# Quarter sums of a fast up-projection: formed in DRAM ahead of time, or by accumulating loads onto the raw weight buffers

## The chip, the cores and the metric

The kernel runs on one core of a Trainium2 chip. The metric is the device time of one execution in microseconds (us). Engines are named as in the profile: PE (TensorE), DVE (VectorE), ACT (ScalarE), POOL (GpSimd) and SP (SyncE). DMAs are issued from SP (plain loads and stores) and from POOL (transfers that add to what lies at the destination, and the copies that go with them).

## The reference, cut to what matters

The program is an encoder of two layers over 512 tokens with 1024 channels. Each layer has a mixing half (one input projection, a convolution, three kinds of attention, gates, an output projection) and a feed-forward half. The change is in the feed-forward half:

```python
def _conv_ffn(h, w_up, conv_w, conv_b, w_down):
    u = _depthwise_conv(h @ w_up, conv_w, conv_b)      # w_up: 1024 x 5632
    gate, up = jnp.split(u, 2, axis=-1)                # 2 x 2816 columns
    return (jax.nn.silu(gate) * up) @ w_down
...
x = x + _conv_ffn(_rmsnorm(x, g_ffn[l]), w_up[l], ffn_conv_w[l], ffn_conv_b[l], w_down[l])
```

## The kernel before, in words

**Units.** All weights come in units of 128 x 1024 float32 (512 KB). `weights` (lines 225 to 254) loads a unit into a raw buffer by a DMA on SP (line 246), ACT writes its rounded high part `w_hi` (line 250), and DVE writes the remainder `w_lo = w_raw - w_hi` (line 252). A product is three matmuls (high by high, high by low, low by high). `unit` keeps two units ahead of the one in use (`LOOK = 2`), and `w_hi` and `w_lo` have three buffers each. So the split of a unit can begin when PE is done with the unit three places earlier. There are two raw buffers `w_raw`; the feed-forward half has two more under the tag `w_more`.

**The up-projection.** Its 5632 output columns are worked in 11 groups g of 512 (two blocks of 128 gate columns and the two blocks of up columns that go with them). Groups 0, 1 and 7 to 10 are computed plainly: four units each, called whole units (`block`, lines 289 to 296), of 24 matmuls with 512 columns. Groups 2 to 6 (`SEVEN`) use a fast scheme with seven products instead of eight: the weights of a group are cut into four quarters A11, A12, A21, A22 (rows and columns of a 2 x 2 split), and the seven products use the three quarters A11, A12, A22 and four sums S1 to S4 of quarters. `seven` (lines 972 to 1020) does one of them: 24 matmuls with 256 columns (line 989), then what ACT and DVE have to do with the result. In sums, with the signs already in the packed weights:

- S3 = A11 + A21, S2 = S3 + A22, S4 = S2 + A12
- S1 = A22 + A21

**Where the sums come from.** `quarter_sums` (lines 1111 to 1132) makes them in DRAM. For each of the five groups and each of the four sums POOL issues one DMA that copies 512 KB and one that adds another 512 KB: 40 DMAs for a layer. `weights` then loads a sum like any other unit (`w_raw<-qS`).

**Work in the background.** The down-projection uses a scheme of the same kind, and its sums are also made in DRAM: `weight_sums` (lines 1134 to 1161), 24 POOL DMAs for a layer of up to 1 MB each, into the tiles `sums`. Both generators stand in one chain in the list `slow`, the quarter sums first (line 1432). `tick` (lines 877 to 895) is called several times in each piece of PE work. It adds `pace` to an account, and while the account is positive it takes the next DMA from the list, which costs 4 for a quarter sum and 11 for a weight sum. Each such DMA waits for the last matmul issued so far (`paced`), so that it starts at its place in PE's work. `pace` is 4.0 and then 2.7 in the mixing half, 0.8 in the seven-product groups, and 2.7 in the whole groups that follow (lines 1062 and 1065).

**The order of the up-projection** is the list `UP_STEPS` (lines 39 to 53): one group after the other, in a seven-product group S3, A11, A22, S2, A12, S1, S4; the last product of a group stands behind the first of the next.

**Behind the up-projection.** The result of a step goes from PSUM through `U` (line 1069 for whole units) and `conv_part` (lines 1022 to 1047) to the gated products `f`, and `split_pair` (lines 1180 to 1217) prepares those for the down-projection. `down` (line 1219) starts with units that hold a quarter of `w_down` and one of the sums (`w_raw<-sums`), and its first products need four PSUM banks of the kind `mm`, the ones that the last up units used.

Of the kernel before, what the change touches and what calls it, by code (L numbers as in the profile page):

```python
# [14 lines left out]
F32 = mybir.dt.float32  # L15
F32R = mybir.dt.float32r
# [6 lines left out]
P = 128  # L23
# [15 lines left out]
def up_steps():  # L39

    steps, held = [], []
    for g in range(NP2):
        if g in SEVEN:
            own = [('seven', g, n) for n in ('S3', 'A11', 'A22', 'S2', 'A12', 'S1', 'S4')]
        else:
            own = [('whole', 2 * g + i, s) for i in range(2) for s in range(2)]
        steps += own[:1] + held
        held = own[-1:] if g in SEVEN else []
        steps += own[1:len(own) - len(held)]
    return steps  # L50
# [166 lines left out]
class Trunk:  # L217
# [7 lines left out]
    def weights(self, upto, ahead=3000, parts=1, queue=None):  # L225

        nc = self.nc
        while self.w_emitted < min(upto, len(self.w_list)):
            n, pieces = self.w_list[self.w_emitted]
            with self.tc.high_priority(offset=ahead):  # L230

                self.w_fast = (self.w_fast + 1) % 4 if n < 2 else 0
                if n == 0 and self.w_fast in (3, 0) or n == 1 and self.w_fast % 2 == 1:
                    raw = self.fp.tile([P, 1024], F32, name="w_raw", tag="w_more", bufs=2)
                else:
                    raw = self.wpool.tile([P, 1024], F32, name="w_raw", tag="w_raw", bufs=2)
# [812 lines left out]
    def ffn(self, l, last):  # L1049
# [9 lines left out]
        self.seven_forms()  # L1059
        for kind, a, b in UP_STEPS:  # L1060
            if kind == 'seven':
                self.pace = 0.8
                self.seven(a, b)
            else:
                self.pace = 2.7 if a > 2 * SEVEN[-1] else 0.0
                ps = self.mm()
                self.block(ps)
                self.tick()
                v.tensor_tensor(self.U[b][:, a % 2, 1:513], ps, self.RB, ALU.mult)  # L1069
# [41 lines left out]
    def quarter_sums(self, l):  # L1111

        dma = lambda *a, **k: self.paced(self.nc.gpsimd.dma_start(*a, **k))  # L1113
        q, t = self.quarters[l], self.qsums[l]
        for g in SEVEN:
            for n in ('S1', 'S2', 'S3', 'S4'):
                t[g, n] = self.dram.tile([P, 1040], F32, name=f"q{n}{g}", tag=f"q{n}{g}", bufs=2)[:, :1024]
        for n, a in (('S3', (1, 0)), ('S1', (1, 1))):
            for g in SEVEN:
                dma(t[g, n], q[(g,) + a])  # L1120
                yield 4
        for n, a in (('S3', (0, 0)), ('S1', (1, 0))):
            for g in SEVEN:
                dma(t[g, n], q[(g,) + a], accum_op=ALU.add)
                yield 4
        for n, m, a in (('S2', 'S3', (1, 1)), ('S4', 'S2', (0, 1))):
            for g in SEVEN:
                dma(t[g, n], t[g, m])
                yield 4
            for g in SEVEN:  # L1130
                dma(t[g, n], q[(g,) + a], accum_op=ALU.add)
                yield 4
# [193 lines left out]
    def run(self):  # L1326
        nc, tc = self.nc, self.tc
        with ExitStack() as st:
# [8 lines left out]
            self.quads, self.sums, self.all_quads, self.quarters, self.qsums = [], [], [], [], []  # L1337
            self.halves = {}
            for l in range(L):
                off, quads, quarters, ups, sums = 0, [], {}, {}, {}  # L1340
# [11 lines left out]
                for kind, a, b in UP_STEPS:  # L1352
                    if kind == 'whole':
                        self.w_list.append((1024, lambda src=ups[b * DFF + a * P]: [src]))
                    elif b[0] == 'A':
                        self.w_list.append((1, lambda src=quarters[a, int(b[1]) - 1, int(b[2]) - 1]: [src]))
                    else:
                        self.w_list.append((1, lambda s=sums, at=(a, b): [s[at]]))
                self.quarters.append(quarters)
                self.qsums.append(sums)  # L1360
# [52 lines left out]
    def layer(self, l):  # L1413
# [3 lines left out]
        with tc.tile_pool(name="gate", bufs=1, reuse_waits="tile") as self.gp:  # L1417
            with tc.tile_pool(name="attn", bufs=1, reuse_waits="tile") as self.ap:
# [13 lines left out]
                self.slow.append(chain(self.quarter_sums(l), self.weight_sums(l)))  # L1432
# [102 lines left out]
```

## Time and profile before

| | before |
|---|---|
| runs, us | 1571.79, 1564.55, 1564.35 |
| median, us | 1564.55 |
| the profiled execution's own time, us | 1565.39 |
| its span in the profile, us | 1563.6 |
| PE busy in the span, us | 1542.8 |
| DVE busy, us | 1250.6 |
| ACT busy, us | 894.0 |
| moved by DMA, MB | 306.84 |

The span runs from the first to the last instruction, and the execution's own time is 1.8 us longer. PE counts as busy while a matmul is under way, and its matmuls overlap: one with 256 columns shows 283 ns and starts about 120 ns after the one before. The granted clock of PE stands in the windows view; 1.00 is full speed. The time of a DMA "to landing" runs from its issue on SP or POOL to the event that tells that it is complete.

### The profile page before, as it was taken

To read this page: it belongs to the slowest core of one execution; us is meant where nothing else is said; L and a number is where in the kernel's file an instruction comes from. 1 tells how busy PE (TensorE), PEld (TensorE's weight loads), DVE (VectorE), ACT (ScalarE), POOL (GpSimd) and SP (SyncE) were. 2 spreads that over 40 slices of the span, in tenths; PEclk is the share of its full clock that TensorE was granted. 3 is DMA by queue.
4 is the path that set the end of the run, shared out by engine and by line. 5 is a ranking of instruction groups with operands and counts; after the bars stand their busy time and mean duration, and the time that the engine had idled before them with its cause. 6 is when DMAs were issued, how large, how long until landed. Compare 5 with 4: busy or idle time off the path is not lost.

```text
span 1563.6 us, 21943 instructions
## 1 busy us (share of the span) xinstructions
PE 1542.8 (99%) x7842; PEld 1310.0 (84%) x7842; DVE 1250.6 (80%) x2114; ACT 894.0 (57%) x1504; POOL 203.4 (13%) x308
## 2 busy tenths in 40 slices
PE   9999999999999999989999999999999999999998
PEld 8888888888789998868888878888888899988787
DVE  6689988764789997986576889887646899999764
ACT  6678767333456664554457677673334566645543
POOL 0133002222100000000002231032221000000000
PEclk9999999999999999999999999999999999999999
DMA  7787765557845868696558977655578469886874
GB/s 239 250 238 211 160 167 156 161 145 164 239 164 145 254 217 162 182 259 203 183 179 272 233 197 158 171 148 169 145 166 249 166 168 276 247 193 181 234 238 160
DMA packets 124797, 306.84 MB, mean 196 GB/s; under 512 B 28176, under 2 KB 30096, under 8 KB 124688
## 3 DMA queue, kind: packets, MB, share of 16 engines
q1 hardware_dynamic: 93712, 212.10, 41.7%
q0 software_dynamic: 30688, 92.81, 28.1%
q8 instruction: 62, 1.02, 0.3%
q10 hardware_dynamic: 288, 0.52, 0.1%
q14 instruction: 47, 0.39, 0.1%
HBM read 287.56 MB, written 100.67 MB: 248 GB/s over the span
## 4 chain that ended last, share of the span: by engine, by line
PE 79%; DVE 9%; DMA 7%; ACT 4%; issue 1%; POOL 0%; ACTq 0%; DVEq 0%; POOLq 0%; SPq 0%
PE mm L272 14%; PE mm L271 14%; PE mm L273 14%; PE aux L989 10%; DMA w_raw<-W 4%; DVE w_lo L252 3%; PE aux L1226 2%; PE aux L1227 2%; PE aux L1228 2%; PE mm L500 2%; PE mm L502 2%; PE mm L501 2%; PE mm L1227 2%; PE mm L1226 2%; PE mm L989 2%; PE mm L1228 2%
## 5 line engine op out<-in xcount | busy, mean ns | idle before, releaser
L250 ACT ACTIVATE w_hi<-w_raw 128x1024 fp32r<-128x1024 f32 (+1 forms) x335 | 350.5, 1047 | 391.0 <-PE mm L272 137.4
L252 DVE TENSOR_TENSOR w_lo<-w_raw,w_hi 128x1024 fp32r<-128x1024 f32 (+1 forms) x335 | 405.9, 1212 | 124.3 <-ACT w_hi L250 122.2
L271 PE MATMUL mm<-xh,w_hi 128*128 128x512 f32 x960 | 375.3, 391 | 1.2 <-DVE V L628 1.2
L273 PE MATMUL mm<-xh,w_lo 128*128 128x512 f32 x960 | 374.4, 390 | 0.3 <-DVE w_lo L252 0.3
L272 PE MATMUL mm<-xl,w_hi 128*128 128x512 f32 x960 | 374.2, 390 | 0.0
L273 PEld LDWEIGHTS mm<-xh,w_lo 128*128 128x128 f32 x960 | 180.2, 188 | 39.6 <-DVE w_lo L252 1.5
L271 PEld LDWEIGHTS mm<-xh,w_hi 128*128 128x128 f32 x960 | 180.3, 188 | 38.0 <-DVE V L628 1.6
L272 PEld LDWEIGHTS mm<-xl,w_hi 128*128 128x128 f32 x960 | 180.3, 188 | 36.0
L989 PE MATMUL aux<-form,w_hi 128*128 128x256 f32 x640 | 116.3, 283 | 0.1
L989 PEld LDWEIGHTS aux<-form,w_hi 128*128 128x128 f32 x640 | 99.9, 192 | 0.5 <-ACT sv L1001 0.3
L438 DVE SCALAR_TENSOR_TENSOR cv<-cv,prm 128x512 f32<-128x512 f32 x120 | 94.1, 784 | 0.7
L989 PE MATMUL aux<-form,w_lo 128*128 128x256 f32 x320 | 90.5, 283 | 0.0
L869 POOL TENSOR_TENSOR mx<-mx,t 128x512 f32<-128x512 f32 x44 | 65.7, 1502 | 174.7 <-DVE t L868 174.7
L1030 ACT ACTIVATE cy<-U,prm 128x512 f32<-128x512 f32 x88 | 68.8, 808 | 29.2 <-DVE U L1069 21.6
L839 DVE TENSOR_TENSOR t<-mm,RB 128x512 f32<-128x512 f32 x64 | 43.9, 686 | 42.6 <-PE mm L273 42.4
L500 PE MATMUL mm<-w_hi,xh 128*128 128x512 f32 x192 | 76.4, 398 | 0.4 <-DVE V L628 0.4
L501 PE MATMUL mm<-w_lo,xh 128*128 128x512 f32 x192 | 75.0, 390 | 0.0
L502 PE MATMUL mm<-w_hi,xl 128*128 128x512 f32 x192 | 74.7, 390 | 0.0
L1113 POOL DMA_DIRECT2D qS<-W x60 | 43.5, 725 | 235.2 <-PE mm L273 95.2
L1136 POOL DMA_DIRECT2D sums<-W x36 | 31.8, 906 | 318.2 <-PE mm L273 153.8
L757 ACT ACTIVATE e<-e,rl 128x256 f32<-128x256 f32 (+2 forms) x96 | 57.3, 597 | 22.4 <-DVE rl L756 22.0
L1031 DVE SCALAR_TENSOR_TENSOR cy<-U,prm,cy 128x512 f32<-128x512 f32 x88 | 64.2, 747 | 2.1 <-ACT cy L1030 2.1
(339 smaller groups left out, 3225.8 us busy)
## 6 DMA issues: line engine op xcount, KB each, us to landing
w_raw<-W SPq DMA_DIRECT2D x213, 512.0 KB, 4.2
qS<-W POOLq DMA_DIRECT2D x60, 512.0 KB, 7.1
sums<-W POOLq DMA_DIRECT2D x24, 1024.0 KB, 11.6
w_raw<-qS SPq DMA_DIRECT2D x40, 512.0 KB, 4.6
w_raw<-W SPq DMA_DIRECT2D x66, 256.0 KB, 3.8
w_raw<-sums SPq DMA_DIRECT2D x22, 512.0 KB, 5.1
w_raw<-sums SPq DMA_DIRECT2D x44, 256.0 KB, 3.8
qS<-qS POOLq DMA_DIRECT2D x20, 512.0 KB, 4.5
```

The lines of the kernel that those rows point to most:

```text
L250: w = nc.scalar.activation(hi[:, s], raw[:, s], AF.Copy)
L252: nc.vector.tensor_tensor(lo[:, s], raw[:, s], hi[:, s].bitcast(F32), ALU.subtract)
L271: mm(ps, lhsT=wh, rhs=xh, start=start, stop=False)
L272: mm(ps, lhsT=wh, rhs=xl, start=False, stop=False)
L273: self.last_mm = mm(ps, lhsT=wl, rhs=xh, start=False, stop=stop)
L438: self.after_mm(v.scalar_tensor_tensor(acc, u[:, t:t + S], w(t), acc, ALU.mult, ALU.add))
L500: mm(pss[b], lhsT=self.Xh[k][:, t], rhs=hi[:, s], start=k == 0, stop=False)
L501: mm(pss[b], lhsT=self.Xh[k][:, t], rhs=lo[:, s], start=False, stop=False)
L502: self.last_mm = mm(pss[b], lhsT=self.Xl[k][:, t], rhs=hi[:, s], start=False, stop=k == KT - 1)
L869: (v if n == ORDER[3] and d >= 6 else nc.gpsimd).tensor_tensor(m, m, t, ALU.add)
L989: self.last_mm = nc.tensor.matmul(o, lhsT=w[:, s], rhs=x, start=start and not (e or j or i), stop=j == 3 and i == 2, skip_group_check=True)
L1030: nc.scalar.activation(y, u[:, 1:513], AF.Identity, scale=w(1), bias=self.par('ffn_conv_b', c))
```

## The change

1. `quarter_sums` is gone, with its 80 POOL DMAs and the DRAM tiles `qS`. `weight_sums` alone stands in `slow`, and `pace` is 0 in the whole feed-forward half.
2. A sum is now formed in the raw buffer. The new `seven_unit` loads A11 into a buffer called `chain` (tag `w_more`, two of them) and A22 and A12 into `w_raw`, by DMAs on SP. After the split of a unit has read the buffer, `grow` issues one DMA on POOL that adds the next quarter from DRAM onto the same buffer: A11 becomes S3, then S2, then S4 in one `chain` buffer; A22 becomes S1 in its `w_raw` buffer. There are four such DMAs in a group, 40 in the program.
3. `UP_STEPS` is written from a table of slots. Group i of the five has A11, S3, A22, S2, A12, S1, S4 at the places 0, 4, 6, 8, 9, 10, 12, counted from 7 i. So neighbouring groups interleave, and S3, S2 and S4 follow the unit from which they grow by four places. The first A11 stands ahead of the last two whole units of group 1. The first two whole units of group 7 are computed inside the last seven-product group, and their PSUM banks are kept (`held`) and emptied after that group (`free`).

```diff
 def up_steps():
 
-    steps, held = [], []
-    for g in range(NP2):
-        if g in SEVEN:
-            own = [('seven', g, n) for n in ('S3', 'A11', 'A22', 'S2', 'A12', 'S1', 'S4')]
-        else:
-            own = [('whole', 2 * g + i, s) for i in range(2) for s in range(2)]
-        steps += own[:1] + held
-        held = own[-1:] if g in SEVEN else []
-        steps += own[1:len(own) - len(held)]
-    return steps
+    whole = lambda g: [('whole', 2 * g + i, s) for i in range(2) for s in range(2)]
+    slots = {}
+    for i, g in enumerate(SEVEN):
+        for n, at in (('A11', 0), ('S3', 4), ('A22', 6), ('S2', 8), ('A12', 9), ('S1', 10), ('S4', 12)):
+            slots[7 * i + at] = ('seven', g, n)
+    steps = [w for g in range(SEVEN[0]) for w in whole(g)]
+    after = [w for g in range(SEVEN[-1] + 1, NP2) for w in whole(g)]
+    own = [slots[t] for t in sorted(slots)]
+    late = [('held',) + w[1:] for w in after[:2]]
+    own = own[:-4] + late[:1] + own[-4:-1] + late[1:] + own[-1:]
+    return steps[:-2] + own[:1] + steps[-2:] + own[1:] + [('free',) + w[1:] for w in after[:2]] + after[2:]
...
             n, pieces = self.w_list[self.w_emitted]
+            if n == 'seven':
+                with self.tc.high_priority(offset=ahead):
+                    self.w_ready.append(self.seven_unit(*pieces))
+                self.w_emitted += 1
+                continue
...
+        held = {}
+        self.pace = 0.0
         for kind, a, b in UP_STEPS:
             if kind == 'seven':
-                self.pace = 0.8
                 self.seven(a, b)
+                continue
+            if kind == 'free':
+                ps = held.pop((a, b))
             else:
-                self.pace = 2.7 if a > 2 * SEVEN[-1] else 0.0
                 ps = self.mm()
                 self.block(ps)
                 self.tick()
+            if kind == 'held':
+                held[a, b] = ps
+            else:
                 v.tensor_tensor(self.U[b][:, a % 2, 1:513], ps, self.RB, ALU.mult)
                 self.conv_part(a, b)
...
-    def quarter_sums(self, l):
...
-        for n, a in (('S3', (0, 0)), ('S1', (1, 0))):
-            for g in SEVEN:
-                dma(t[g, n], q[(g,) + a], accum_op=ALU.add)
-                yield 4
...
+    def grow(self, raw, src):
+        self.nc.gpsimd.dma_start(raw, src, accum_op=ALU.add)
+
+    def seven_unit(self, l, g, n):
+
+        nc = self.nc
+        q = lambda r, c: self.quarters[l][g, r - 1, c - 1]
+        if n[0] == 'A':
+            if n == 'A11':
+                raw = self.fp.tile([P, 1024], F32, name="chain", tag="w_more", bufs=2)
+            else:
+                raw = self.wpool.tile([P, 1024], F32, name="w_raw", tag="w_raw", bufs=2)
+            nc.sync.dma_start(raw, q(int(n[1]), int(n[2])))
+            self.raws[g, n] = raw
+        else:
+            raw = self.raws[g, 'A22' if n == 'S1' else 'A11']
+        hi = self.wpool.tile([P, 1024], F32R, name="w_hi", tag="w_hi", bufs=3)
+        lo = self.wpool.tile([P, 1024], F32R, name="w_lo", tag="w_lo", bufs=3)
+        nc.scalar.activation(hi, raw, AF.Copy)
+        nc.vector.tensor_tensor(lo, raw, hi.bitcast(F32), ALU.subtract)
+        more = {'A11': (2, 1), 'S3': (2, 2), 'S2': (1, 2), 'A22': (2, 1)}.get(n)
+        if more:
+            self.grow(raw, q(*more))
+        return hi, lo
...
-                self.slow.append(chain(self.quarter_sums(l), self.weight_sums(l)))
+                self.slow.append(self.weight_sums(l))
```

POOL's instructions where the feed-forward half of layer 0 begins, before: `xf<-res` is the last of eight loads that start that half, `sums` are the three DRAM tiles of the down-projection's sums.

```order
L940 DMA xf<-res_4187 128x512
L1136 DMA sums_3011<-W 512x512
L1136 DMA sums_3012<-W 384x512
L1136 DMA sums_3010<-sums_3010 512x512
L1136 DMA sums_3011<-sums_3011 512x512
L1136 DMA sums_3012<-sums_3012 384x512
```

The same place after the change, with the numbers of the buffers: each `chain` number is the buffer of one group, `w_raw` here is the buffer in which A22 becomes S1.

```order
L946 DMA xf_4505<-res7_4141 128x512
L1124 DMA chain_4767<-W 128x1024 x2
L1124 DMA w_raw_4913<-W 128x1024
L1124 DMA chain_4946<-W 128x1024
L1124 DMA chain_4767<-W 128x1024
L1124 DMA chain_4946<-W 128x1024
L1124 DMA w_raw_5148<-W 128x1024
```

The weight sums, of which 14 of the 24 stood behind the `xf` loads in each layer, now all stand ahead of them, and in the feed-forward half POOL issues only the accumulating loads.

DVE's instructions in the middle of the seven-product groups of layer 0, before: `w_lo` is the second half of a unit's split, `cy0` and `cy1` belong to the convolution, and L1018 empties the PSUM bank of an S4.

```order
L252 TENSOR_TENSOR w_lo_5461<-w_raw_5459,w_hi_5460 128x1024
L1031 SCALAR_TENSOR_TENSOR cy0_5371<-U0_4536,prm_73,cy0_5371 128x512
L1031 SCALAR_TENSOR_TENSOR cy0_5377<-U0_4536,prm_73,cy0_5377 128x512
L1032 SCALAR_TENSOR_TENSOR cy0_5371<-U0_4536,prm_73,cy0_5371 128x512
L252 TENSOR_TENSOR w_lo_5493<-w_raw_5491,w_hi_5492 128x1024
L1032 SCALAR_TENSOR_TENSOR cy0_5377<-U0_4536,prm_73,cy0_5377 128x512
L1018 TENSOR_TENSOR U1_4539<-aux_5208,RB_4598 128x2x256
L252 TENSOR_TENSOR w_lo_5523<-w_raw_5521,w_hi_5522 128x1024
```

The corresponding place after the change: the three splits are those of an A22 (`w_raw`), of the A11 of the group after it, and of an S2 (`chain_4946`).

```order
L1142 TENSOR_TENSOR w_lo_5151<-w_raw_5148,w_hi_5150 128x1024
L1037 SCALAR_TENSOR_TENSOR cy0_5105<-U0_4490,prm_73,cy0_5105 128x512
L1037 SCALAR_TENSOR_TENSOR cy0_5111<-U0_4490,prm_73,cy0_5111 128x512
L1038 SCALAR_TENSOR_TENSOR cy0_5105<-U0_4490,prm_73,cy0_5105 128x512
L1142 TENSOR_TENSOR w_lo_5194<-chain_5191,w_hi_5193 128x1024
L1038 SCALAR_TENSOR_TENSOR cy0_5111<-U0_4490,prm_73,cy0_5111 128x512
L1024 TENSOR_TENSOR U1_4493<-aux_4805,RB_4552 128x2x256
L1142 TENSOR_TENSOR w_lo_5224<-chain_4946,w_hi_5223 128x1024
```

DVE's work has kept its kinds, its number and nearly its order. What has changed is where a split's input comes from: before from two raw buffers that SP fills ahead, now in four of seven cases from a buffer that an earlier split has read and a POOL DMA has since added to.

More of the change, by code (lines that the diff above doesn't have):

```diff
@@ L229, in weights @@
             n, pieces = self.w_list[self.w_emitted]
+            if n == 'seven':
[3 more added lines that the diff above has]
+                continue
             with self.tc.high_priority(offset=ahead):
-                self.w_fast = (self.w_fast + 1) % 4 if n < 2 else 0
-                if n == 0 and self.w_fast in (3, 0) or n == 1 and self.w_fast % 2 == 1:
+                self.w_fast = (self.w_fast + 1) % 4 if n == 0 else 0
+                if n == 0 and self.w_fast in (3, 0):
                     raw = self.fp.tile([P, 1024], F32, name="w_raw", tag="w_more", bufs=2)
@@ L1109, in last_units @@
         self.w_list.extend((0, u) for u in units)
-    def quarter_sums(self, l):
-        dma = lambda *a, **k: self.paced(self.nc.gpsimd.dma_start(*a, **k))
-        q, t = self.quarters[l], self.qsums[l]
-        for g in SEVEN:
[L1116 to L1120, printed above, removed]
-                yield 4
-        for n, a in (('S3', (0, 0)), ('S1', (1, 0))):
-            for g in SEVEN:
-                dma(t[g, n], q[(g,) + a], accum_op=ALU.add)
[L1125 to L1132, printed above, removed]
+    def grow(self, raw, src):
[20 more added lines that the diff above has]
+        return hi, lo
     def weight_sums(self, l):
@@ L1336, in run @@
             self.w_list = []
-            self.quads, self.sums, self.all_quads, self.quarters, self.qsums = [], [], [], [], []
-            self.halves = {}
+            self.quads, self.sums, self.all_quads, self.quarters = [], [], [], []
+            self.halves, self.raws = {}, {}
             for l in range(L):
-                off, quads, quarters, ups, sums = 0, [], {}, {}, {}
+                off, quads, quarters, ups = 0, [], {}, {}
                 for kind, a, n in UNITS:
@@ L1352, in run @@
                 for kind, a, b in UP_STEPS:
-                    if kind == 'whole':
+                    if kind == 'seven':
+                        self.w_list.append((kind, (l, a, b)))
+                    elif kind != 'free':
                         self.w_list.append((1024, lambda src=ups[b * DFF + a * P]: [src]))
[L1355 to L1358, printed above, removed]
                 self.quarters.append(quarters)
-                self.qsums.append(sums)
                 self.quads.append(quads)
```

## The prediction

> **What bounds the kernel now.** I read the page first: the span and the busy times.
>
> ```profile
> span 1563.6 us, 21943 instructions
> PE 1542.8 (99%) x7842; PEld 1310.0 (84%) x7842; DVE 1250.6 (80%) x2114; ACT 894.0 (57%) x1504; POOL 203.4 (13%) x308
> ```
>
> PE is busy all but 20.8 us. The change keeps every matmul, so a gain can only come out of those 20.8 us and out of a lowered clock. The waits of PE say where they lie.
>
> ```profile
> PE mm L1226 <- DVE U L1069: 5.7, 1, 5.7
> PE aux L732 <- DVE pt L778: 3.1, 5, 1.5
> PE mm L1226 <- ACT w_hi L250: 1.5, 1, 1.5
> PE mm L1227 <- DVE w_lo L252: 1.4, 2, 0.8
> ```
>
> L1226 and L1227 are the first matmuls of the down-projection; L732 is in the attention. The windows view, with the two seven-product stretches first and then the two passages from up to down (us, PE, PEld, DVE, ACT, POOL busy, clock, DMA share, GB/s):
>
> ```profile
> 480.00:581.00 101.00, 101.00 (x831) 100.43 (x831) 96.04 (x126) 65.76 (x86) 3.91 (x5) 1.00 0.73 213
> 1258.00:1359.00 101.00, 100.87 (x829) 100.15 (x828) 96.33 (x125) 64.61 (x83) 3.94 (x5) 1.00 0.84 239
> 669.00:685.00 16.00, 10.32 (x38) 8.06 (x38) 12.25 (x19) 10.22 (x15) 2.00 (x2) 0.79 1.00 217
> 1462.00:1478.00 16.00, 13.11 (x48) 9.79 (x47) 8.50 (x15) 5.89 (x9) 0.00 (x0) 0.89 0.85 256
> ```
>
> In the seven-product stretches PE does not wait at all, so there the change can only lose; but DVE is at 95%. At the passages PE stands idle 5.7 and 2.9 us, and the clock falls to 0.79 and 0.89 of full speed over 16 us, which costs another 0.21 x 16 = 3.4 and 0.11 x 16 = 1.8 us. Together 9.1 us in layer 0 and 4.7 in layer 1: 13.8 us are to be had there at most.
>
> The chain of waits shows what ends last there, in layer 0 and in layer 1 (start, length, what):
>
> ```profile
> 661.02 9.64 DMA w_raw<-sums
> 670.76 1.07 ACT w_hi L250
> 671.86 1.23 DVE w_lo L252
> 676.72 0.61 DVE U L1069
> 677.38 0.79 PE mm L1226
> ...
> 1448.12 10.36 DMA U<-resT
> 1458.53 15.30 DMA w_raw<-sums
> 1473.94 1.07 ACT w_hi L250
> 1475.03 1.24 DVE w_lo L252
> 1476.31 0.50 PE mm L1227
> ```
>
> In both layers it is a load of a weight sum, and it is slow because of POOL's last weight sums beside it. Their rows, layer 0 and layer 1 (durations on POOL in ns, then landing), and under them the loads of a quiet stretch and of one with a weight sum in flight:
>
> ```profile
> L1136 POOL DMA_DIRECT2D sums<-W x3: 1037/1068/1364, 659.2 to 670.7; - x3
> DMA to landing us min/median/max: 11.7/12.1/15.5
> ...
> L1136 POOL DMA_DIRECT2D sums<-W x3: 1050/1053/1381, 1438.8 to 1450.3; - x3
> DMA to landing us min/median/max: 14.4/16.6/22.4
> ...
> L246 SPq DMA_DIRECT2D w_raw<-qS x3: 319/326/326, 483.1 to 494.6; - x3
> DMA to landing us min/median/max: 3.3/3.4/4.2
> ...
> L246 SPq DMA_DIRECT2D w_raw<-qS x3: 320/326/327, 500.2 to 506.3; - x3
> DMA to landing us min/median/max: 6.3/8.2/9.5
> ```
>
> A 512 KB load takes 3.4 us alone and 8.2 us beside a weight sum.
>
> **The passages.** The change sets `pace` to 0 in the feed-forward half and has 160 units of account less in front of the weight sums, so by the order of POOL all 24 of a layer are issued before that half begins. Nothing of them is left at 659 or 1439. Layer 0: the load issued at 661.0 then lands after about 3.4 us, at 664.5 and not 670.8. DVE had run dry waiting for it:
>
> ```profile
> 671.86 1.23 DVE L252 TENSOR_TENSOR w_lo<-w_raw,w_hi 128x1024 fp32r<-128x1024 f32 x1 [3.76 <-ACT w_hi L250]
> ```
>
> Without the 3.8 us DVE empties the last up unit's bank (U, L1069) at 673.5 instead of 677.3. PE still waits 5.7 - 3.8 = 1.9 us for it, because DVE has the split and parts of two pair preparations in front, and those stay in that order. The clock's 3.4 us I count as regained: 7.2 us. Bounds: 3.8 + 1.6 = 5.4 if as much clock is lost as layer 1 shows (1.8), and the whole 9.1.
>
> On the clock the trace and a rule disagree. In layer 1 PE stood still 2.9 us in all, never over 1.5 at a stretch by the list of waits, and the clock fell all the same. The Trainium skill, "TensorE: Matmul & The Clock Gate", section "Why this matters for your kernels", wants no idle gap over about 3 us between bursts and has the clock halved after one idle window; by it a rest of 1.9 us would leave the clock alone and the sum as it is, by the row of layer 1 it would cost 1.8 us more.
>
> Layer 1: the same load falls away as a brake, but `U<-resT` (10.4 us) stays and shares the DMA engines with the loads. I take 3.5 of the 4.7 us; bounds 0 and 4.7. Passages together: 10.7 us, between 5.4 and 13.8.
>
> **The seven-product stretch.** What is new is a chain: split, POOL DMA onto the buffer, next split. A unit takes 101 us / 35 = 2.89 us of PE. The costs of a split and of an accumulating DMA (in DRAM, the nearest rows: four in a stretch with little else, ten back to back in a stretch whose DMA share the windows view puts above 1):
>
> ```profile
> L250 ACT ACTIVATE w_hi<-w_raw 128x1024 fp32r<-128x1024 f32 (+1 forms) x335 | 350.5, 1047 | 391.0 <-PE mm L272 137.4
> L252 DVE TENSOR_TENSOR w_lo<-w_raw,w_hi 128x1024 fp32r<-128x1024 f32 (+1 forms) x335 | 405.9, 1212 | 124.3 <-ACT w_hi L250 122.2
> ...
> L1113 POOL DMA_DIRECT2D qS<-W x4: 802/806/821, 159.2 to 183.1; - x4
> DMA to landing us min/median/max: 5.0/6.8/7.4
> ...
> L1113 POOL DMA_DIRECT2D qS<-W x10: 812/814/902, 92.2 to 125.1; - x10
> DMA to landing us min/median/max: 6.2/8.1/9.1
> ...
> 93.00:127.00 34.00, 32.86 (x169) 27.22 (x168) 30.19 (x63) 22.21 (x51) 7.49 (x10) 1.00 1.04 249
> ```
>
> A split is 1.05 + 1.21, with hand-overs 2.5 us. With a landing of L a link takes L + 2.5, and links stand four units apart: 11.6 us. A `chain` buffer is used for a reload (3.4 + 2.5 = 5.9 us) and three links in 14 units, 40.5 us, before the group after next needs it. So 5.9 + 3 (L + 2.5) may not exceed 40.5: L up to 9.0. At 6.8 the buffer's round takes 33.8, at 8.1 it takes 37.7 us. The accumulating DMAs come one in 5.0 us (20.2 us / 4), less dense than the ten above (one in 3.5 us) and with three plain loads in a group instead of seven; I take 6.8. PE is not held up then. A split also cannot be early (three `w_hi` buffers, so two units ahead), and with DVE's 5 us of slack in 101 a DVE that waits for a late DMA cannot make much good: I book 1 us for the program, between 0 and the price of the rival below.
>
> For the DMA itself the skill gives less: the Trainium skill, "DMA: Bandwidth & Descriptors", section "Anatomy of one DMA — SWDGE (gpsimd) path", fits 2.0 us plus the bytes at 436 GB/s, an estimate of 3.2 us for 512 KB. The rows above show 5.0 to 9.1 for transfers that add, so the measurement decides; by the skill's figure the booking would be 0 and the sum 1 us lower.
>
> In the same stretch POOL issues no weight sums any more, so plain loads are no longer at 8.2 us. The POOL queue holds nothing but these DMAs there, so what waits behind a blocked one is only the next of its kind; behind it wait ACT and DVE with the next split. On SP the reload of a `chain` buffer waits for the S4 split two units before its need, and the loads of A12 and A22 queue behind it, but they are wanted later. The two held units put 48 matmuls that leave DVE nothing but their two splits at the end of the stretch, which helps DVE; cost 0, and if PSUM ran short, the wait would show at L271.
>
> **The mixing half.** 40 DMAs of 512 KB per layer leave it and 14 of up to 1 MB enter, so the bytes are nearly equal; by the account a MB of weight sums takes 11 and a MB of quarter sums 8 units, so the beginning is less dense. One load there took very long, and waits at L732 follow it:
>
> ```profile
> 896.43 16.87 DMA w_raw<-W
> ```
>
> It may get shorter, or a 1 MB transfer may hit another load. I take 0, between -3 (the 3.1 us at L732) and +3.
>
> **Sum.** -10.7 + 1 + 0 = -9.7 us: a span of 1553.9. The profiled execution's own time was 1565.4, 0.8 above the median of the runs; I go by the median, 1564.55, and forecast 1554.9. A change of 0.5% is 7.8 us, about what a measurement of this kernel can tell from none.
>
> **The rivals.**
>
> *The chain binds (slower).* For it: the accumulation onto an SBUF buffer is in no row here, DVE is nearly full, and in layer 1 the stretch has a DMA share of 0.84 already. Each us of L above 9.0 costs 3 us in a buffer's round, of which there are 2.5 in a layer: 15 us for the program. It eats the gain at L = 9.7 and makes the kernel slower by more than 0.5% from 10.2. Price at 10.5: 22.5 us, 1576. Against: of the 14 rows above none is over 9.1, and a sustained mean would have to be.
>
> *The gain does not come (no change).* Something else is as late at the passages: the bank of the last up unit behind DVE's pair preparations in layer 0, `U<-resT` in layer 1. Then the gain is the 3.8 + 1.6 us of layer 0 less 1 to 3 us of small waits in the seven-product stretch, about 3 us: 1561.5. For it: with the load gone, DVE's queue is 1.9 us behind PE by my own sum. The same time comes out if L is about 9.4 with the gain in full.
>
> *More is gained.* Loads in the mixing half also get shorter, and the whole 13.8 us are regained: 1564.5 - 13.8 - 1 = 1549.7.
>
> **How the numbers follow.** The forecast has 0.60, of which 0.05 lies within 0.5%; more gained 0.05; no change 0.22; the chain binds 0.13. So faster 0.55 + 0.05 = 0.60, the same 0.05 + 0.22 = 0.27, slower 0.13. The range runs from the gain in full with part of the mixing half, 1549, to 1567, past the second rival and the first part of the first; what it leaves out is about 0.13 above and 0.05 below. The forecast's own range is 1550.5 to 1558.
>
> **What the profile of the changed kernel would show.** Right: no `sums` DMA after the `xf` loads; the `w_raw<-sums` loads at the passage land in 3 to 6 us; PE's 5.7 us at L1226 shrinks to about 2 and the clock over the passage of layer 0 is above 0.9; landings of the accumulating loads of 5.5 to 8 us; both seven-product stretches (now with two whole units in them) without waits of PE for `w_hi` or `w_lo`. Wrong: PE or PEld waiting at the seven-product line for the new splits, ACT waiting several us at a time for DMAs onto `chain`, landings above 9 us; or a passage that still shows 5 us with another releaser.

## The result, and the profile after

| | before | after |
|---|---|---|
| median of the runs (lowest to highest), us | 1564.55 | 1550.3 (1549.82 to 1552.27) |
| profiled execution, us | 1565.39 | 1550.59 |
| its span, us | 1563.6 | 1548.7 |
| PE busy in the span, us | 1542.8 | 1538.4 |
| moved by DMA, MB | 306.84 | 264.87 |

The ratio of after to before is 0.990, with a 95% interval of 0.987 to 0.993. The kernel became faster by 14.3 us, 1% of its time, where 9.7 were forecast. Ratios here and below compare fast runs alone; one of the four executions of the first experiment took 5026.69 us and is not among them.

The first lines of the page and PE's waits, after:

```profile
span 1548.7 us, 21808 instructions
PE 1538.4 (99%) x7842; PEld 1309.5 (85%) x7842; DVE 1247.6 (81%) x2114; ACT 896.7 (58%) x1504; POOL 183.8 (12%) x268
...
PE mm L277 <- ACT mh L879: 2.7, 1, 2.7
...
PE aux L738 <- DVE pt L784: 0.3, 1, 0.3
```

The waits at the down-projection's first matmuls (L1240 and L1241 after, L1226 and L1227 before) are gone from the list, and so are those of the attention (3.1 us before, now 0.3). In their place stands one wait of 2.7 us, for `mh`, the input of layer 0's output projection. The seven-product stretches and the passages in the windows view (us, then PE, PEld, DVE, ACT and POOL busy, clock, DMA share, GB/s):

```profile
464.00:584.00 120.00, 119.99 (x901) 115.46 (x900) 110.09 (x149) 75.67 (x97) 17.53 (x20) 1.00 0.73 159
1231.00:1352.00 121.00, 120.98 (x906) 116.12 (x904) 114.10 (x154) 74.98 (x96) 17.50 (x20) 1.00 0.86 185
666.00:682.00 16.00, 16.00 (x73) 13.24 (x72) 15.14 (x24) 12.18 (x18) 0.00 (x0) 1.00 0.45 138
1452.00:1468.00 16.00, 16.00 (x73) 13.23 (x72) 16.00 (x29) 10.48 (x16) 0.00 (x0) 1.00 0.62 196
```

PE is busy throughout in all four, at full clock. At the passages POOL's DMAs are gone, and the DMA share fell from 1.00 and 0.85 to 0.45 and 0.62. The DMAs behind this, each with the time to landing (minimum, median, maximum): the loads over the passage of layer 0, the loads of `resT` over that of layer 1, and the accumulating loads of the whole program, all after; in the second fence the loads of `resT` before.

```profile
L252 SPq DMA_DIRECT2D w_raw<-sums x5: 320/425/433, 663.6 to 680.2; - x5
L252 SPq DMA_DIRECT2D w_raw<-W x3: 332/333/333, 663.3 to 679.8; - x3
DMA to landing us min/median/max: 3.0/3.7/5.3
...
L1261 SPq DMA_DIRECT2D U<-resT x4: 319/428/647, 1438.9 to 1446.6; - x4
DMA to landing us min/median/max: 3.9/4.6/5.0
...
L1124 POOL DMA_DIRECT2D chain<-W x30: 872/872/911, 464.9 to 1341.9; - x30
L1124 POOL DMA_DIRECT2D w_raw<-W x10: 863/872/891, 483.9 to 1335.9; - x10
DMA to landing us min/median/max: 5.4/5.8/8.7
```

```profile
L1247 SPq DMA_DIRECT2D U<-resT x4: 320/462/735, 1448.1 to 1455.9; - x4
DMA to landing us min/median/max: 10.4/14.4/16.7
```

**Where the 14.9 us of span come from.** Outside the seven-product stretches PE's order is the same in both kernels, so the start of the same matmul can be compared in the two traces. The last column is what the difference grew by since the row above it.

| matmul in | before, us | after, us | difference | change |
|---|---|---|---|---|
| mixing half of layer 0 | 335.82 | 334.75 | -1.07 | -1.1 |
| output projection of layer 0 | 428.82 | 431.80 | +2.98 | **+4.1** |
| last whole group, layer 0 | 631.74 | 634.14 | +2.41 | -0.6 |
| down-projection, layer 0 | 710.62 | 705.32 | -5.31 | **-7.7** |
| mixing half of layer 1, behind its first attention | 965.43 | 955.94 | -9.49 | **-4.2** |
| first whole groups, layer 1 | 1225.39 | 1215.69 | -9.70 | -0.2 |
| last whole groups, layer 1 | 1408.27 | 1399.04 | -9.23 | +0.5 |
| down-projection, layer 1 | 1504.62 | 1489.71 | -14.91 | **-5.7** |

The passages gave 13.4 us. The mixing halves gave 1.4 in sum, out of -4.2 in one place, +4.1 in another, and two small ones. The up-projection cost nothing: -0.6 in layer 0 and +0.5 in layer 1.

### The profile page after: what moved, and what is told of

The parts are those of the page before. It is cut to its first block, busy times and chain, and to the rows that moved or that the text cites. A ratio compares the mean times of both kernels' runs of the same rounds, so it can differ in the third digit from the quotient of the medians.

```text
span 1548.7 us, 21808 instructions
## 1 busy us (share of the span) xinstructions
PE 1538.4 (99%) x7842; PEld 1309.5 (85%) x7842; DVE 1247.6 (81%) x2114; ACT 896.7 (58%) x1504; POOL 183.8 (12%) x268
## 2 busy tenths in 40 slices
DMA packets 113275, 264.87 MB, mean 171 GB/s; under 512 B 26896, under 2 KB 28816, under 8 KB 113168
## 4 chain that ended last, share of the span: by engine, by line
PE 87%; DVE 5%; DMA 4%; ACT 3%; issue 1%; POOL 0%; DVEq 0%; ACTq 0%; POOLq 0%
PE mm L278 16%; PE mm L279 16%; PE mm L277 16%; PE aux L995 7%; PE aux L1242 3%; PE aux L1241 3%; PE aux L1240 3%; PE mm L506 2%; PE mm L507 2%; PE mm L508 2%; DMA w_raw<-W 2%; PE mm L1242 2%; PE mm L1241 2%; PE mm L1240 2%; PE aux L799 2%; PE aux L776 2%
## 5 line engine op out<-in xcount | busy, mean ns | idle before, releaser
L256 ACT ACTIVATE w_hi<-w_raw 128x1024 fp32r<-128x1024 f32 (+1 forms) x265 | 276.8, 1044 | 318.0 <-PE mm L278 151.1
L258 DVE TENSOR_TENSOR w_lo<-w_raw,w_hi 128x1024 fp32r<-128x1024 f32 (+1 forms) x265 | 320.0, 1209 | 91.5 <-ACT w_hi L256 89.8
L1037 DVE SCALAR_TENSOR_TENSOR cy<-U,prm,cy 128x512 f32<-128x512 f32 x88 | 63.7, 744 | 1.4 <-ACT cy L1036 1.4
L1038 DVE SCALAR_TENSOR_TENSOR cy<-U,prm,cy 128x512 f32<-128x512 f32 x88 | 64.6, 744 | 0.3
```

Of the source, the lines that this page charges most:

```text
L256: w = nc.scalar.activation(hi[:, s], raw[:, s], AF.Copy)
L258: nc.vector.tensor_tensor(lo[:, s], raw[:, s], hi[:, s].bitcast(F32), ALU.subtract)
```

## The experiments

Theory A, from here on: the gain is that no weight sum runs in the feed-forward half any more; the accumulating loads neither gain nor cost. Theory B: the gain comes from 42 MB less traffic and the new order of the units.

**1. One half of the change without the other.** First, the kernel before, with all background transfers ahead of the feed-forward half (the costs 4 and 11 stand four times each):

```diff
-                yield 4
+                yield 2.5
...
-                yield 11
+                yield 6.8
...
-                self.pace = 0.8
-                self.pace = 2.7 if a > 2 * SEVEN[-1] else 0.0
+                self.pace = 0.0
```

> The kernel before with its quarter sums in DRAM, but with the costs in the account lowered from 4 and 11 to 2.5 and 6.8, so that all 64 background transfers of a layer are issued before the feed-forward half, in which pace is 0. No accumulating load, old order of the units. Theory A: the passages alone give 13.4 us, less up to 5 us for a mixing half with 42 MB more in it than the changed kernel's: 1551 to 1556 us. Theory B (less traffic and the new order make the gain): 1562 to 1567 us. A third outcome: the denser mixing half loses more than the passages give, over 1567 us, with loads there that land in over 12 us and PE waiting in the attention or the output projection.

Measured: 1549.44 us, ratio 0.990 (0.986 to 0.993): the whole gain of the change, without any accumulating load, with 306.84 MB moved as before and in the old order of the units. Theory B falls. The windows over the same two passages in this run:

```profile
664.00:680.00 16.00, 16.00 (x72) 13.28 (x71) 15.27 (x24) 12.31 (x18) 0.00 (x0) 1.00 0.44 141
1450.00:1466.00 16.00, 16.00 (x72) 13.27 (x71) 16.00 (x29) 10.54 (x16) 0.00 (x0) 1.00 0.60 196
```

By the starts of the same matmuls, the passages gave 7.6 and 5.7 us against the kernel before, where the changed kernel has 7.7 and 5.7. I had feared that a denser mixing half would give some of it back; it lost 1.3 us in layer 0 and gained 3.4 in layer 1's attention.

Second, the changed kernel with the weight sums late, as before:

```diff
-                self.pace, self.served = 4.0, -40.0
+                self.pace, self.served = 4.0, -200.0
...
             if kind == 'seven':
+                self.pace = 0.8
                 self.seven(a, b)
...
+                self.pace = 2.7 if kind == 'whole' and a > 2 * SEVEN[-1] else 0.0
                 ps = self.mm()
```

> The changed kernel with the weight sums where they stood before: 10 of a layer's 24 ahead of the feed-forward half, 14 inside it, with the pace of the kernel before (0.8 and 2.7). The accumulating loads stay. Theory A, the gain is the weight sums' place: the losses at the two passages come back, 13.4 us of the 14.9 us by which the profiled spans differ, so 1560 to 1567 us, PE waiting 4 us or more at the first matmuls of the down-projection in at least one layer, and loads of sums that land in 8 us or more there. Theory B, the gain comes from 42 MB less traffic and the new order of the units: it stays, 1549 to 1553 us. Theory C, weight sums beside the accumulating loads lengthen these beyond 9 us and the chain of the quarters binds: over 1570 us, with PE waiting in the seven-product stretches.

Measured: 1598.64 us, ratio 1.021 (1.019 to 1.024). This is theory C's time (what delays the stretch is the subject of part 2), 48 us over the changed kernel. The losses at the passages come back (10.8 and 9.8 us between the same matmuls), and both up-projections lose as well (13.0 and 18.9 us). Against that, 6.4 us are gained on the way to the output projection of layer 0.

Third, the changed kernel without the accumulating loads:

```diff
-        if more:
-            self.grow(raw, q(*more))
```

> The changed kernel without the 40 accumulating loads: the units S1 to S4 are split from the buffer as it is, so the sums are left out of the computation. The order of the units and everything else stay. Theory A, the chain lies wholly beside other work: 1549.3 to 1551 us, the same within 1 us. Theory B, the chain costs something that other gains have hidden in the total: 1545 to 1548 us.

Measured: 1550.08 us, ratio 0.990 (0.988 to 0.993). The spans differ by 0.7 us, of which 0.6 lie in the up-projection of layer 1. So the chain costs 0.7 us at most in the changed kernel.

**2. Why late weight sums hurt the new order so much.** The late kernel without accumulating loads (the two edits above together):

> The kernel of the run with late weight sums (14 of 24 inside the feed-forward half, 1598.6 us), without the 40 accumulating loads: S1 to S4 are split from the buffers as they are, so those sums are left out. It tells what of the 48 us that the late weight sums cost is the chain. Theory A: only the passages' loss stays, 13 to 15 us, so 1562 to 1566 us, and 33 us or so were the chain, whose accumulating loads stand beside weight sums. Theory B: the new order of the units and its two raw buffers suffer from weight sums even without the chain: over 1580 us.

Measured: 1583.68 us, ratio 1.011 (1.009 to 1.013). I had expected the chain to be 33 us or so of the 48; it is 15. So theory A falls for this run, and theory B has the time: 8.8 us in layer 0 and 9.9 us in layer 1 are lost in the up-projection with no accumulating load anywhere. The chain of waits there, in layer 0:

```profile
497.92 9.72 DMA chain<-W
...
507.73 1.06 ACT w_hi L1143
...
522.78 8.05 DMA chain<-W
...
530.92 1.06 ACT w_hi L1143
```

These are plain loads of an A11 on SP. They take 9.7 and 8.1 us because a weight sum was issued about 2 and 4 us earlier, as it also happened before; but they are issued only when S4's split has released the buffer, and nothing is left to cover them. To test that, S4 is split from another buffer, so that the `chain` buffer is free four units earlier (this run too leaves the sums out):

```diff
-            raw = self.raws[g, 'A22' if n == 'S1' else 'A11']
+            raw = self.raws[g, {'S1': 'A22', 'S4': 'A12'}.get(n, 'A11')]
```

> The kernel of the run with late weight sums and without accumulating loads (1583.7 us), with one more edit: S4 is split from the buffer of A12 in place of the chain buffer (the sums are left out anyway), so that a chain buffer is free for its reload after S2, four units (11.6 us) earlier. In the run before it, 18.7 us were lost in the two seven-product stretches. Theory A, they were lost because the reload of a chain buffer can be issued only some 10 us before its need, and takes 8 to 10 us beside a weight sum: they go, 1562 to 1568 us, and only the passages' losses stay. Theory B, something else in the new order suffers from the weight sums: still over 1578 us.

Measured: 1573.70 us, ratio 1.007 (1.005 to 1.009). The seven-product stretch of layer 0, without this edit, and with it (with a row for the passage behind it):

```profile
478.00:598.00 120.00, 114.82 (x872) 111.41 (x871) 102.15 (x135) 69.97 (x90) 3.92 (x5) 0.97 0.44 117
```

```profile
478.00:598.00 120.00, 118.99 (x907) 114.65 (x905) 106.54 (x140) 73.19 (x95) 3.92 (x5) 1.00 0.46 121
670.00:702.00 32.00, 24.80 (x97) 19.48 (x98) 23.78 (x41) 15.46 (x21) 0.56 (x1) 0.93 1.05 254
```

From the head of the stretch to behind the last of those waits, the matmuls now keep their distance to those of the changed kernel within 0.1 us, in both layers. With their buffers free earlier, the same reloads are issued ahead of the weight sum and land in 3.5 to 4.4 us in layer 0. So the late reload was the cause. The time is 6 us above the upper end of what I expected, because the whole groups and the passage behind the stretch lose 13.6 us in layer 0 and 14.2 in layer 1 here: the weight sums that are left over are issued in a burst at the end of the up-projection, and the DMA share over the passage is 1.05.

**3. How much room the chain has.** The accumulating loads issued twice:

```diff
-        self.nc.gpsimd.dma_start(raw, src, accum_op=ALU.add)
+        for _ in range(2):
+            self.nc.gpsimd.dma_start(raw, src, accum_op=ALU.add)
```

> The changed kernel with each accumulating load issued twice, one behind the other (the quarter is added twice, which the reference does not want). The link gets longer by one landing, from 5.6 to about 11.3 us. By the account of the prediction (9.0 us are free, above that 15 us of program for each us of the link) 34 us are lost: 1580 to 1590 us, with PE waiting in both seven-product stretches for splits from the chain buffers. Rival: a split may be two units early and a buffer's round has more slack than I counted, so that less than half of it is lost: under 1566 us. Second rival: the doubled traffic on POOL's queue makes even the plain loads late: over 1600 us.

Measured: 1665.54 us, ratio 1.064 (1.062 to 1.067). The direction was right, and the size wrong by far: 115 us in place of 34, or 11.8 us in each of the ten groups by the trace. The time is that of the second rival, and the plain loads of the stretches did land later, in 5.7 us at the median where the changed kernel has 4.6. POOL's instructions of this run show what the account had left out (start, length, and in brackets the idle time before and who ended it):

```profile
486.45 0.88 POOL L1125 DMA_DIRECT2D chain<-W  x1 [4.85 <-DMA chain<-W]
487.20 1.04 POOL L1125 DMA_DIRECT2D w_raw<-W  x1
494.78 0.87 POOL L1125 DMA_DIRECT2D w_raw<-W  x1 [6.54 <-DMA w_raw<-W]
495.31 2.17 POOL L1125 DMA_DIRECT2D chain<-W  x2
503.17 0.87 POOL L1125 DMA_DIRECT2D chain<-W  x1 [5.69 <-DMA chain<-W]
```

The second addition of a pair waits on POOL for the first to land, and what stands behind it in POOL's order waits with it. From the first issue of a pair to the second is 8.3 us on the mean, so four pairs in a group fill POOL's queue for up to 33 us, against 20.2 us of PE work; the group took 20.2 + 11.8 = 32.0. But the links were longer as well: from the first issue of a pair to its second landing the trace has 15.1 us on the mean, not 11.3, and 15.1 + 2.5 us in every four units alone would make a group of about 31 us. This run doesn't separate the two. The account had doubled a quiet landing, and had left out the queue and the longer landings of the doubled traffic.

The second way to a longer landing, the same 512 KB in smaller pieces (`k` = 8, then 4):

```diff
-        self.nc.gpsimd.dma_start(raw, src, accum_op=ALU.add)
+        c = 1024 // k
+        src = self.all_quads[len(self.sums) - 1][:P].rearrange("p (i c) -> p i c", c=2 * c)[:, :, :c]
+        self.nc.gpsimd.dma_start(raw.rearrange("p (i c) -> p i c", c=c), src, accum_op=ALU.add)
```

> The changed kernel with accumulating loads of the same 512 KB, but read from DRAM in pieces of 512 bytes with gaps between them (from another place of W, so the sums are other sums than the reference's). One landing gets longer, with nothing more on POOL's queue. By the account of the prediction the time is 1550.3 + 15 us for each us of the mean landing above 9.0. Rival account: each of the 30 links of the chains is four units, 11.6 us, from the next, so that a landing above 9.1 costs 30 us for each us. Should the landing stay under 9 us, both say 1549 to 1551.5.

Measured: 1623.68 us, ratio 1.037 (1.034 to 1.040), with a median landing of only 6.5 us and a mean of 7.1. Both accounts said no loss; both fall. POOL again:

```profile
520.14 1.46 POOL L1126 DMA_DIRECT2D chain<-W  x1 [5.45 <-DVE cy L1037]
526.76 1.46 POOL L1126 DMA_DIRECT2D chain<-W  x1 [5.17 <-DMA chain<-W]
533.40 1.46 POOL L1126 DMA_DIRECT2D chain<-W  x1 [5.18 <-issue]
539.94 1.46 POOL L1126 DMA_DIRECT2D w_raw<-W  x1 [5.08 <-DVE cy L1037]
```

One issue in 6.5 to 6.7 us: about one landing apart, whatever the row names as the releaser. In the whole trace none of the 40 comes sooner than 0.3 us behind the landing of the one before. In the changed kernel, two such issues can stand as little as 1.1 to 2.4 us apart (510.83 and 513.22, for instance). Four in a group make 26.7 us, 6.5 over PE's 20.2, or 65 us for ten groups; the spans differ by 70.7. So here it is POOL's queue, with one accumulating load under way at a time. Why POOL holds the next one back with these pieces, the runs do not show.

> The same with pieces of 1024 bytes, for a landing between that of the changed kernel and that of the 512-byte pieces. The same two accounts: 1550.3 + 15 us, or + 30 us, for each us of the mean landing above 9; under 9 us, 1549 to 1551.5.

Measured: 1554.43 us, ratio 0.994 (0.991 to 0.996); mean landing 6.2, median 5.9 us. All of the loss lies in layer 1, and 3.6 of its 4.6 us at one place. In the chain of waits there:

```profile
1313.52 6.85 DMA chain<-W
...
1324.31 9.98 DMA chain<-W
```

The first row is a plain reload of a `chain` buffer by SP, and PE stalls right behind it, from 1320.4 us; in the changed kernel the same reload took 5.2 us and cost nothing. The second is the slowest accumulating load of the run, 10.0 us, and in the 17 us behind its landing no matmul falls further back. So for one late link the account of the prediction (room for 9 us and a little over) is not contradicted, and the thin place is the reload once more.

Then the spacing of the links, by the table of slots:

```diff
-        for n, at in (('A11', 0), ('S3', 4), ('A22', 6), ('S2', 8), ('A12', 9), ('S1', 10), ('S4', 12)):
+        for n, at in (('A11', 0), ('S3', 3), ('A22', 4), ('A12', 5), ('S2', 6), ('S1', 8), ('S4', 9)):
```

> The changed kernel with another table of slots: A11, S3, A22, A12, S2, S1, S4 at 0, 3, 4, 5, 6, 8, 9, so the links of a chain stand three units (8.7 us) apart in place of four (11.6). Theory A, a link takes its landing plus 2.5 us, with the landings of the changed kernel's profile (median 5.7, most under 7): 8.2 us on the median, so it just fits: 1549 to 1555 us, small waits where a landing is above 6.2. Rival, the two units' lead of a split is used up by ACT and DVE, which work in order and stand still behind a split whose buffer is late: over 1565 us.

Measured: 1562.53 us, ratio 0.998 (0.997 to 0.999): 12 us over the changed kernel, between theory and rival. The landings were no longer than expected (median 5.6, maximum 7.2 us). The loss comes in pieces of 0.6 to 0.8 us, one in nearly every group, and larger ones in layer 1. So a link takes more than landing plus 2.5 us. ACT and DVE have other work in front of a split when it becomes due, which I think is the reason; no run here takes that work away.

```diff
+        for n, at in (('A11', 0), ('A12', 1), ('S3', 2), ('A22', 3), ('S2', 4), ('S1', 5), ('S4', 6)):
```

> The changed kernel with the groups one after the other again (A11, A12, S3, A22, S2, S1, S4 at 0 to 6), the accumulating loads kept. The links stand two units apart, 5.8 us. Theory A, the interleaving is what pays for the latency: a link takes 8.2 us, three links and one unit make 27.5 us of a group in place of 20.2, so 7 us in each of ten groups and a lowered clock on top: 1610 to 1650 us. Rival, the lead of two units absorbs it: under 1565 us.

Measured: 1605.62 us, ratio 1.026 (1.024 to 1.028): 55 us over the changed kernel, a little under what was expected. The list of PE's waits of this run names the splits first, and behind them ACT's copies out of PSUM (`sv`):

```profile
PE aux L995 <- ACT w_hi L1141: 25.2, 11, 3.6
PE aux L995 <- ACT sv L1007: 10.1, 5, 3.0
```

With the groups one after the other the accumulating loads would have made the kernel 41 us slower than before. The interleaving pays for them.

Last, the two held units taken out of the stretch:

```diff
-    late = [('held',) + w[1:] for w in after[:2]]
-    own = own[:-4] + late[:1] + own[-4:-1] + late[1:] + own[-1:]
-    return steps[:-2] + own[:1] + steps[-2:] + own[1:] + [('free',) + w[1:] for w in after[:2]] + after[2:]
+    return steps[:-2] + own[:1] + steps[-2:] + own[1:] + after
```

> The changed kernel without the two units of group 7 inside the seven-product stretch, so that in the last seven-product group two links stand three units apart in place of four. Theory A: 2 to 6 us lost (three units apart in all five groups cost 12 us): 1552 to 1556 us. Rival: the lead of a split absorbs it: 1549 to 1551.5 us.

Measured: 1554.97 us, ratio 0.993 (0.991 to 0.995), 4.7 us over the changed kernel, as theory A had it. The held units keep the last group's links four apart.

**4. The two places in the mixing half.** The changed kernel with its weight sums a little denser:

```diff
-                yield 11
+                yield 10
```

> The changed kernel with a cost of 10 in place of 11 for each weight sum, so that each is issued earlier and the last one of layer 0 at about 350 us, not 379. Theory A, the 3.7 us that the changed kernel loses before the output projection of layer 0 (PE waits 2.7 us for mh, and runs at a lower clock) come from the last two weight sums beside the loads there: these go, 1546 to 1548.5 us, with loads at 365 to 395 us that land in under 5 us. Theory B, the loads there are late for another reason: the same 1550 within 1 us. Third outcome: the denser transfers hit loads elsewhere in the mixing half: over 1551 us.

Measured: 1547.56 us (1547.15 to 1548.46), ratio 0.989 (0.986 to 0.991). Theory A. This is the fastest version here: none of its runs is as slow as any of the changed kernel's, 1549.82 to 1552.27, at a kernel before of 1564.6 in both series. In the chain of waits of the changed kernel, the place that it mends:

```profile
367.69 11.75 DMA w_raw<-W
...
381.87 10.36 DMA w_raw<-W
...
392.33 1.07 ACT w_hi L256
...
396.69 0.64 ACT mh L879
...
398.10 0.80 PE mm L278
398.89 0.43 PE mm L279
```

And the loads over that place in this run, six of them:

```profile
L252 SPq DMA_DIRECT2D w_raw<-W x6: 327/328/328, 365.3 to 390.6; - x6
...
DMA to landing us min/median/max: 3.4/3.5/4.8
```

The kernel before, with its quarter sums' additions spread:

```diff
-                dma(t[g, n], q[(g,) + a])
-                yield 4
+                dma(t[g, n], q[(g,) + a])
+                yield 2
...
-                dma(t[g, n], q[(g,) + a], accum_op=ALU.add)
-                yield 4
+                dma(t[g, n], q[(g,) + a], accum_op=ALU.add)
+                yield 6
```

> The kernel before with the same transfers in the same order, but the quarter sums' copies cost 2 and their additions 6 in the account, not 4 each, so that the additions are issued 1.5 times as far apart and the weight sums stand where they stood. Theory A, the 4.2 us that the changed kernel gained in the attention of layer 1 came from the ten additions in a row there, which no longer slow a load to 16.9 us: 1559 to 1562 us, the passages as before. Theory B, that load was slow for another reason: 1564 to 1566 us. Third outcome: the copies, twice as dense, slow other loads: over 1567 us.

Measured: 1571.76 us, ratio 1.005 (1.003 to 1.006). By its total this is the third outcome, but the place under test did what theory A said: from the first attention of layer 1 to the matmul behind it, 3.9 us were gained, and the load that had taken 16.87 us takes 8.5. The copies, now issued twice as densely, cost 5.6 us at the first attention of layer 0, with a new wait of 2.7 us for a load of `V`, and later places lose another 2. Since the edit also shifted the loads and additions of layer 1 against each other, it makes the spacing the likeliest reason there, not the only possible one.

## Why the prediction was right and wrong

The mechanism that the sum rests on was right: late weight sums slow the loads at the passages. So was the direction. The size was not: the time, 1550.3 us, stands near the low end of the range and just outside the forecast's own 1550.5 to 1558, and the gain is 1.5 times the forecast.

The step that failed is what the prediction left standing at the passages: 1.9 us of PE's wait in layer 0, and in layer 1 the 1.2 of 4.7 us that it kept for `U<-resT`. Nothing stayed. PE is busy through both passages at a clock of 1.00, in the changed kernel and in the old one with early weight sums. The term that was most mis-sized by it is the passage of layer 1, with 3.5 us booked and 5.7 measured. By spans 14.9 us were gained in place of 9.7. Of these 5.2 us more, 2.2 are layer 1's passage, 1.4 the mixing halves (booked at 0), 1.1 the seven-product stretch (booked as 1 us lost, measured as 0.1 gained) and 0.5 the passage of layer 0. The outcome lies nearer to the rival "more is gained", 1549.7 us, to which I gave 0.05, than to the forecast of 1554.9. (That rival takes its last 1 us off without a row for it, where the sum books 1 us lost.) Step by step:

- **The passage of layer 0** (forecast 7.2, measured 7.7 us): right in size by luck, out of two errors that nearly cancel. The first: I had PE still waiting 1.9 us for the last up unit's bank, since I took the 3.76 us of DVE's idle time for all that the slow loads had cost DVE. The `U` two units ahead shows more. In the kernel before it begins without having waited for PE; with the weight sums early (the second fence, from the first experiment, where PE stands within 0.2 us of the kernel before) DVE waits there for PE:

```profile
662.36 0.69 DVE L1069 TENSOR_TENSOR U<-mm,RB 128x512 f32<-128x512 f32 x1
664.09 1.23 DVE L252 TENSOR_TENSOR w_lo<-w_raw,w_hi 128x1024 fp32r<-128x1024 f32 x1 [1.05 <-ACT w_hi L250]
```

```profile
658.96 0.69 DVE L1068 TENSOR_TENSOR U<-mm,RB 128x512 f32<-128x512 f32 x1 [1.85 <-PE mm L273]
659.87 1.23 DVE L252 TENSOR_TENSOR w_lo<-w_raw,w_hi 128x1024 fp32r<-128x1024 f32 x1 [0.22 <-ACT w_hi L250]
```

  DVE was already 3.4 us late there, so all 5.7 us of PE's wait came back, not 3.8. The second error is the price of the clock. I multiplied its mean loss, 0.21, by all 16 us of the window. Two shorter windows of the kernel before, in the same columns, show that PE stood still for half of the time at the low clock:

```profile
674.00:677.40 3.40, 0.02 (x1) 0.02 (x1) 3.30 (x8) 2.67 (x5) 0.00 (x0) 0.50 1.07 196
677.40:681.00 3.60, 3.60 (x9) 2.88 (x10) 3.60 (x5) 2.73 (x5) 0.00 (x0) 0.53 1.07 247
```

  A low clock costs nothing while PE waits. The matmuls lost 7.6 us there; without the wait of 5.7 that leaves 1.9 us for the clock, not 3.4. The second rival ("something else is as late") rested on the same 1.9 us, and fell with it.
- **The passage of layer 1** (forecast 3.5 with bounds 0 and 4.7, measured 5.7): the mis-sized term. "`U<-resT` (10.4 us) stays and shares the DMA engines" was wrong: that transfer was itself a victim. It lands in 4.6 us after, 14.4 before, and in 4.7 in the old kernel with its weight sums early (medians). The upper bound was too low as well: the starts of the matmuls show 5.4 us lost inside my window, where its idle time and clock make 4.7, and 0.3 us behind it.
- **The seven-product stretch** (booked +1 us, measured -0.6 in layer 0 and +0.5 in layer 1; without the accumulating loads 0.7 us less): right within its bounds. The landing was 5.8 us at the median, where I took 6.8. The trace's minimum, 5.4 us, is well above the estimate of 3.2 us by the fit in the Trainium skill's "DMA: Bandwidth & Descriptors", section "Anatomy of one DMA — SWDGE (gpsimd) path".
- **The account behind the rival "the chain binds"** was wrong in what it left out. Landings above 9.0 us were its only trigger. The runs show three others that come first: POOL's queue (four issues have to fit into 20.2 us; 73 us in the run with 512-byte pieces, and a part of the 115 us of the doubled loads), the reload of a `chain` buffer beside a weight sum (19 us), and the spacing (12 us lost where the account still had 0.6 us of room in each link). I had written that the reload waits for S4's split, and did not ask what a slow one would cost. In the changed kernel none of this is reached, because nothing else runs on POOL and no weight sum is there. So the rival did not come true, but the change is safe only as a whole: its `pace = 0` is a condition of its `chain` buffers and accumulating loads (with late weight sums its up-projections lose 13.0 and 18.9 us), not a side effect.
- **The mixing half** (0, between -3 and +3; measured -1.4): inside the bounds as a sum, which hides two changes of 4 us each. A load of 16.87 us stood beside the dense additions of the quarter sums in layer 1; experiment 4, which spread them, won 3.9 us there. The last two weight sums of layer 0 now stand beside the loads ahead of the output projection, and with the weight sums issued sooner that loss is gone. I had named the first, and had not looked where the last weight sums would stand. That the bytes are nearly equal was wrong too: 40 transfers of 512 KB are 20 MB, and 14 of up to 1 MB at most 14; it is the units of the account that are, 160 and 154.
- **The clock.** The longest wait that is left, 2.7 us for `mh`, is followed by matmuls that take 0.43 us of the chain of waits above, where one takes 0.23 otherwise. The section "Why this matters for your kernels" of the Trainium skill's "TensorE: Matmul & The Clock Gate" warns of gaps over about 3 us. This trace shows the lower clock after 2.7 us, and the trace before shows it in layer 1 after two gaps close together, of 1.5 and 0.8 us. At the passages themselves no gap is left and the clock is 1.00, so that nothing there hung on the rule.

What stays open: why POOL issues accumulating loads in 512-byte pieces one landing apart, what share of the 115 us of the doubled loads is the queue, and the exact length of a link, which lies between three and four units at these landings.

## What to carry to other kernels

When a change has two halves, price them apart: here the gain was the background traffic's place, to be had with a few numbers in the old kernel, and the new way of making the sums gained nothing by itself. A slow transfer in the row of a chain of waits is often not alone: ask which other late rows nearby have the same cause before you book them as what remains. And a buffer that is read, added to and read again turns every transfer that touches it, and the queue that issues it, into a link of one chain; count the queue's issues in a period as well as one link's latency.

## What the runs showed of the hardware

- An accumulating load of 512 KB onto an SBUF buffer took 5.4 to 8.7 us, median 5.8: like the additions in DRAM in a quiet stretch (5.0 to 7.4). A plain load of 512 KB took 4.6 us at the median beside them, and 3.4 in a quiet stretch of the kernel before.
- The same bytes in 512-byte pieces landed only 0.7 us later at the median (6.5), but POOL issued them 6.5 us apart at the closest, each behind the landing of the one before, where the whole ones came as little as 1.1 us apart.
- One more hint on throughput: the 64 background transfers of a layer, packed into the mixing half, landed in 11.1 us at the median for a quarter sum's 512 KB (7.1 before), and cost PE 1.3 us in layer 0 and less than before in layer 1.
